# Output sums of the first output pair kept in SBUF, one queue step per job

## The chip, the cores and the metric

The kernel runs on one core of a Trainium2 chip. The metric is the device time of one execution in microseconds (us). Three runs of the kernel before took 1672.77, 1674.2 and 1676.46 us, with a median of 1674.2.

## The reference

Two layers run over a sequence of 512 rows of width 2048 (float32). Each layer normalises its input, multiplies it by one wide input matrix, hands the columns to a gated-linear-attention (GLA) group of 4 heads and a chunked-attention group of 8 heads, normalises and gates each head's output, concatenates both groups, multiplies by an output matrix, normalises and adds the input:

```python
h = rmsnorm(x, g_pre)
z = h @ w_in
gq, gk, gv, gg, ga, aq, ak, av, ag = split_columns(z)
...
o_gla = rmsnorm(o_gla, ...) * silu(gg)      # 1024 columns, 4 heads of 256
o_att = rmsnorm(o_att, ...) * silu(ag)      # 1024 columns, 8 heads of 128
y = jnp.concatenate([o_gla, o_att], axis=-1) @ w_out
return x + rmsnorm(y, g_post)
```

The change concerns the last product, `@ w_out`, and the way its left operand reaches TensorE.

## The kernel before

**Products.** The weights are cut into blocks of 512 columns: 14 of `w_in` and 4 of `w_out` for each layer. Float32 precision is had from a split: an operand is a high part (ScalarE's copy to fp32r) and a low part (VectorE's difference), and a product is the sum of three matmuls, high by high, high by low, low by high. The weights' parts are the tiles `wh` and `wl`, with four and three buffers.

**Pairs of blocks.** Most blocks are multiplied two at a time by `fast_gemm`, with a scheme of Strassen's kind: seven products, P1 to P7, on sums of quarter blocks instead of eight on quarter blocks. Each product has four steps over the contraction (0 to 3), so that a pair is 28 *jobs* of 12 matmuls each. A job loads its weights (`Job.load`), adds them where its product needs a sum and casts the high part (`high`), and makes the low part (`low`). Loads run up to five jobs ahead of the matmuls, the other steps three to four (`ahead`). The order of the jobs is written out by hand; for the first output pair it is `PROD_OUT`:

```python
PROD_OUT = order("10 20 11 21 12 13 50 51 60 61 22 23 52 53 62 63 30 31 32 33 70 71 72 73 40 41 42 43")
LEFT = {"P5": "S1", "P6": "S2", "P3": "S4", "P7": "S3", "P4": "A22"}
```

"50" is step 0 of P5. `LEFT` names the left operand: P5, P6, P3 and P7 need a sum, S1, S2, S4 or S3, of quarters of the activations. The four steps of an output pair take the GLA heads in the order `OC` = 2, 3, 0, 1.

**The output sums.** For each step the quarters are a11 and a21 (attention, first and second half of the rows, read from DRAM by `out_parts`) and a12 and a22 (GLA head, first and second half, written by `turn_gla`). S1 = a21 - a22, S2 = S1 - a11, S4 = a12 + S2, S3 = a11 - a21. `make_sums` makes the four of one head after another, as soon as both halves of the head are there; each is one VectorE operation and a split. The result is put into one of the slots g0 to g3, written to DRAM (`so_d`, tile name oS in the profile, on POOL's queue), and read again by the job that needs it into the ring `sa` (four buffers, on SP's queue, line 175). The parts of the four heads share two sets of slots, g9/g10 and g12/g13.

**What runs around it.** Before the output pair the pair PAIRS[5] makes the GLA gates. Its consumer (`gg_consume`) gates the heads, and `turn_gla` transposes them on TensorE (line 1123), 8 or 11 queue steps later. Steps of this kind stand in `tasks` (generators, one step at a time) and `delayed` (a countdown). `Pace` runs `rate` of these steps behind each job; it was 3 in the gate pair and in the output pair. A task was also `residual_rows`, which loads the layer's input rows (12 loads on POOL's queue), needed at the end of the layer in `finish_token` (line 1262). The first output pair gives columns 0 to 1023. The other 1024 come from `std_gemm` in layer 0 and from a second `fast_gemm` (W23) in layer 1, which needs the same sums.

**Order on the engines.** The program's order is not the last word: a planner replays the program against its own durations and sets each engine's order from that. `tc.issue_after(last_cast[0])` keeps a sum's copy behind the newest weight cast on ScalarE.

Of the kernel before, what the change touches and what calls it, by code (L numbers as in the profile page):

```python
# [7 lines left out]
F32 = mybir.dt.float32  # L8
# [3 lines left out]
ALU = mybir.AluOpType  # L12
# [21 lines left out]
def hybrid_trunk(  # L34
# [60 lines left out]
    sa_d = [{(n, c): dram([P, 1024], f"{n}{l}{c}") for n in ("S1", "S2", "S3", "S4", "A22") for c in range(4)} for l in range(L)]  # L95
    so_d = [{(n, c): dram([P, 1024], f"o{n}{l}{c}") for n in ("S1", "S2", "S3", "S4") for c in range(4)} for l in range(L)]
    oa_d = [{(h, c): dram([P, 1024], f"oa{l}{h}{c}") for h in range(2) for c in range(4)} for l in range(L)]
# [39 lines left out]
    class Job:  # L137
# [14 lines left out]
        def load(self):  # L152
            k, c, p, b0, b1 = self.kind, self.c, self.pair, self.b0, self.b1
            end = b0 >= NB_IN and k != "std"
            if end:
                c = OC[c]
            top, bottom = (c + 4, c) if end else (c, c + 4)
            if k == "std":
                self.raw = self.fetch(rtile("raw"), b0, c)
            elif k == "P1":  # L160
                p["H", self.c] = self.fetch(rtile("H"), b0, top)
            elif k == "P5":
                p["r", self.c] = self.fetch(rtile("raw"), b1, top)
            elif k == "P6":
                p["r", self.c] = self.fetch(rtile("raw"), b1, bottom)
            elif k == "P7":
                p["r", self.c] = self.fetch(rtile("raw"), b0, top)
            elif k == "P2" or (k == "P4" and end):
                p["r", self.c] = self.fetch(rtile("raw"), b0, bottom)
            sums = (so_d if end else sa_d)[self.l]  # L170
            src = sums.get((LEFT.get(k), c))
            if src is not None and not (k == "P5" and b0 == AV0):
                until(lambda: k == "P4" or (id(sums), LEFT[k], c) in written)
                self.a = rtile("sa", (2, 512), F32R)
                nc.sync.dma_start(flat(self.a), src)
# [140 lines left out]
    def fast_gemm(l, pair, consume, rate=0.0, skip=0, feature_major=False, after=None, end=False, lag=0, ops=A):  # L316
# [38 lines left out]
        def matmuls(job, k, c, ts):  # L355
            a = job.a
            if a is None:
                key = {"P1": (0, 0, c), "P2": (1, 0, c), "P4": (1, 1, c), "P5": ("S1", c)}[k]
                until(lambda: key in ops)
                a = ops[key]  # L360
# [327 lines left out]
    def layer(l):  # L688
# [416 lines left out]

        parts = {}

        def out_parts(c):
            if c not in parts:
                halves = [slot(tag, [2, 512]) for tag in (("g9", "g10"), ("g12", "g13"))[c % 2]]  # L1110
                parts[c] = [halves[0][:, 0, :], halves[0][:, 1, :], halves[1][:, 0, :], halves[1][:, 1, :]]
                for half in range(2):
                    nc.sync.dma_start(
                        parts[c][2 * half].rearrange("p (k n) -> p k n", k=2),
                        of_att[l][c][:, :, half * 256 : (half + 1) * 256],
                    )
            return parts[c]

        def turn_gla(h, p):
# [17 lines left out]
            og[p, h] = op  # L1137
            O[1, p, OC.index(h)] = op

        def gla_heads(j, gvh, gvl):  # L1140
# [41 lines left out]

        def ready_parts(c):
            return parts[c] if (0, c) in og and (1, c) in og else None

        def gv_consume(j, h, t, src, comb):
# [11 lines left out]
        def gg_consume(j, h, t, src, comb):  # L1198
            until(lambda: len(gla_done) == 4)
            sg = t2()  # L1200
            nc.scalar.activation(sg, settled(src, comb), AF.Silu)
            for i in range(2):
                dst = normed[2 * j + i, h][:, t, :]
                nc.vector.tensor_tensor(out=dst, in0=dst, in1=sg[:, i * 256 : (i + 1) * 256], op=ALU.mult)
                if t:
                    delayed.append([8 + 3 * i, lambda hd=2 * j + i: turn_gla(hd, h)])

        tasks.append(make_sums(so_d[l], ("g0", "g1", "g2", "g3"), ready_parts, chunks=OC))
        fast_gemm(l, PAIRS[5], gg_consume, rate=3, after=fetch_operands)
# [12 lines left out]

        def load_gain(n):
            gp = t2()
            src = g_post[l, n * W : (n + 1) * W]
# [15 lines left out]
        def out_evac(n):  # L1241
            gp = load_gain(n)

# [33 lines left out]

        def residual_rows():
            for half in range(2):
                xs.append(load_tokens(half, x_src, nc.gpsimd))  # L1280
                yield

        tasks.append(residual_rows())

        def out_consume(n):
            gains = [load_gain(n + j) for j in range(2)]

            def f(j, h, t, src, comb):
                o = 2 * h + t
                project(o, n + j, comb(t2()), gains[j])  # L1290
# [7 lines left out]

        fast_gemm(l, W01, out_consume(0), rate=3, end=True, ops=O)
        drain()  # L1300
        if last:
            fast_gemm(l, W23, out_consume(2), rate=3, end=True, lag=3, ops=O)
# [68 lines left out]
```

## Time and profile before

| | |
|---|---|
| median of three runs | 1674.2 us |
| the profiled execution, its time | 1678.37 us |
| its span, first to last instruction | 1676.5 us |
| mean granted TensorE clock | 0.986 |
| TensorE busy | 1622.6 us (97%) |
| VectorE busy | 1261.3 us (75%) |
| ScalarE busy | 908.0 us (54%) |
| POOL busy | 142.5 us (8%) |
| moved by DMA | 451.34 MB, mean 269 GB/s |

In the profile PE is TensorE, PEld its weight loads, DVE VectorE, ACT ScalarE, SP and POOL the engines whose queues issue most of the DMAs. A row of the waits reads: engine, tile and line, what it waited for, total us, times, longest us. A row of the chain reads: start, duration, what. A row of the timeline reads: start, duration, engine, line, operation, output tile <- input tiles, shape, count, and in brackets the idle time before it with what ended it. A row of the windows reads: stretch, its length, then busy us and count of each engine, the granted clock as a share of full speed, the DMA engines' busy share and GB/s. A row of a group ends with busy us and mean ns of one, then idle time. A row of the DMA issues gives count, KB each, and median us to landing. Times are us from the span's start.

### The profile page before, as it was taken

The numbers are of one execution on the slowest core, as the hardware profiler recorded it, in microseconds if no ns is written. First come the engines' busy times: TensorE is split into PE (matmuls) and PEld (weight loads), VectorE is DVE, ScalarE is ACT, GpSimd is POOL, SyncE is SP. The second block draws the span as 40 slices with busy tenths as digits, with TensorE's granted clock in tenths as the row PEclk, the third lists the DMA queues.
The fourth block names the chain that finished last, engine by engine and source line by source line (L and its number), as shares of the span: only waits on it lengthen the run. The fifth ranks groups of instructions, "written<-read, shape, count | busy, mean of one in ns | idle before, by whom it ended". The sixth has DMA issues, their size and how long they took to land.

```text
span 1676.5 us, 24715 instructions
## 1 busy us (share of the span) xinstructions
PE 1622.6 (97%) x8986; PEld 1387.4 (83%) x8986; DVE 1261.3 (75%) x1639; ACT 908.0 (54%) x1494; POOL 142.5 (8%) x216
## 2 busy tenths in 40 slices
PE   9999999999999999599999999999999999996996
PEld 7888999998887778488888889999988877775884
DVE  5977777777687869685786577776776878796878
ACT  7554445666554557354774444455665545573542
POOL 0110000010110111100122000000100000111002
PEclk9999999999999999799999999999999999997998
DMA  8788685875859688986789496858758586889965
GB/s 339 269 343 312 221 294 185 301 267 190 301 191 334 206 278 317 329 326 207 242 280 400 160 323 213 300 179 277 259 191 286 199 317 215 290 322 332 346 225 201
DMA packets 137528, 451.34 MB, mean 269 GB/s; under 512 B 14836, under 2 KB 27508, under 8 KB 137408
## 3 DMA queue, kind: packets, MB, share of 16 engines
q1 hardware_dynamic: 117792, 380.77, 65.6%
q0 software_dynamic: 19040, 67.92, 10.5%
q8 instruction: 71, 1.16, 0.3%
q10 hardware_dynamic: 576, 1.08, 0.2%
q14 instruction: 49, 0.40, 0.1%
HBM read 388.10 MB, written 61.62 MB: 268 GB/s over the span
## 4 chain that ended last, share of the span: by engine, by line
PE 85%; DMA 7%; issue 4%; DVE 2%; POOL 1%; ACT 0%; SPq 0%; DVEq 0%; POOLq 0%; ACTq 0%
PE mm L381 44%; PE mm L302 16%; PE mm L371 16%; DMA raw<-in_w_dram 3%; PE ax L891 2%; DMA sa<-oS 1%; DMA oS<-g 1%; DVE wl L199 1%; PE ax L1072 1%; PE ax L874 1%; PE ax L711 1%; PE ax L1044 1%; PE ax L381 1%; PE ax L855 1%; PE ax L854 1%
## 5 line engine op out<-in xcount | busy, mean ns | idle before, releaser
L381 PE MATMUL mm<-wh,sa 128*128 128x512 f32 x1600 | 523.6, 398 | 34.6 <-DMA sa<-oS 34.6
L199 DVE TENSOR_TENSOR wl<-raw,wh 128x1024 fp32r<-128x1024 f32 (+1 forms) x253 | 306.8, 1216 | 125.8 <-PE mm L381 63.2
L191 ACT CAST wh<-raw 128x1024 fp32r<-128x1024 f32 (+1 forms) x253 | 265.3, 1053 | 244.7 <-PE mm L381 75.8
L381 PEld LDWEIGHTS mm<-wh,sa 128*128 128x128 f32 x1600 | 304.0, 190 | 110.3 <-issue 37.2
L191 ACT CAST wh<-H 128x1024 fp32r<-128x1024 f32 x240 | 251.4, 1050 | 209.9 <-PE mm L381 88.9
L199 DVE TENSOR_TENSOR wl<-H,wh 128x1024 fp32r<-128x1024 f32 x240 | 292.3, 1220 | 88.7 <-PE mm L381 26.2
L381 PE MATMUL mm<-wl,sa 128*128 128x512 f32 x800 | 315.9, 395 | 0.0
L371 PE MATMUL mm<-sa,wh 128*128 128x256 f32 x1280 | 236.9, 285 | 0.5 <-DMA sa<-S 0.5
L381 PE MATMUL mm<-wh,a 128*128 128x512 f32 x608 | 200.4, 394 | 0.0
L371 PEld LDWEIGHTS mm<-sa,wh 128*128 128x128 f32 x1280 | 199.6, 191 | 0.7 <-ACT wh L191 0.6
L371 PE MATMUL mm<-sa,wl 128*128 128x256 f32 x640 | 181.5, 284 | 0.7 <-DVE wl L199 0.6
L381 PEld LDWEIGHTS mm<-wl,sa 128*128 128x128 f32 x800 | 152.2, 190 | 29.9
L185 DVE TENSOR_TENSOR H<-H,raw 128x1024 f32<-128x1024 f32 x132 | 160.4, 1219 | 6.1 <-DMA raw<-in_w_dram 4.8
L381 PEld LDWEIGHTS mm<-wh,a 128*128 128x128 f32 x608 | 113.2, 188 | 23.2
L421 POOL TENSOR_TENSOR sm<-sm,mhalf 128x2 f32<-128x2 f32 (+2 forms) x42 | 54.7, 1302 | 904.6 <-DVE sm L901 452.9
L371 PEld LDWEIGHTS mm<-sa,wl 128*128 128x128 f32 x640 | 122.4, 191 | 1.3 <-DVE wl L199 1.1
L187 DVE TENSOR_TENSOR raw<-H,raw 128x1024 f32<-128x1024 f32 x60 | 73.5, 1224 | 62.2 <-DMA raw<-in_w_dram 61.9
L381 PE MATMUL mm<-wl,a 128*128 128x512 f32 x304 | 120.2, 395 | 0.0
L371 PE MATMUL mm<-a,wh 128*128 128x256 f32 x512 | 95.2, 285 | 0.0
L302 PE MATMUL mm<-wh,a 128*128 128x512 f32 x288 | 91.7, 390 | 0.0
L333 ACT COPY ev<-mm 128x512 f32<-128x512 f32 x96 | 55.9, 584 | 65.9 <-PE mm L381 49.2
L302 PE MATMUL mm<-wh,g 128*128 128x512 f32 x240 | 81.9, 391 | 0.0
(227 smaller groups left out, 2348.3 us busy)
## 6 DMA issues: line engine op xcount, KB each, us to landing
raw<-in_w_dram SPq DMA_DIRECT2D x323, 512.0 KB, 4.8
sa<-S SPq DMA_DIRECT2D x184, 512.0 KB, 4.3
H<-in_w_dram SPq DMA_DIRECT2D x60, 512.0 KB, 4.9
sa<-A SPq DMA_DIRECT2D x48, 512.0 KB, 6.1
sa<-oS SPq DMA_DIRECT2D x48, 512.0 KB, 5.8
S<-g POOLq DMA_DIRECT2D x32, 512.0 KB, 8.6
oS<-g POOLq DMA_DIRECT2D x32, 512.0 KB, 7.4
oa<-g POOLq DMA_DIRECT2D x12, 512.0 KB, 5.7
```

The lines of the kernel that those rows point to most:

```text
L185: nc.vector.tensor_tensor(out=h, in0=h, in1=r, op=ALU.add)
L187: nc.vector.tensor_tensor(out=r, in0=h, in1=r, op=ALU.subtract)
L191: last_cast[0] = nc.scalar.copy(self.wh[:, z, :], src[:, z, :]).ins
L199: nc.vector.tensor_tensor(out=self.wl[:, z, :], in0=self.src[:, z, :], in1=self.wh[:, z, :].bitcast(F32), op=ALU.subtract)
L302: nc.tensor.matmul(pss[o], a(part, kk, o) if callable(a) else a[:, part, t], rhs[:, kk, :], start=(i == 0 and kk == 0 and m == 0), stop=(i ...
L333: nc.scalar.copy(e, src[t])
L371: nc.tensor.matmul(dst, lhs[:, kk, f], a[:, part, tok], start=(fresh and kk == 0 and m == 0 and ft % 2 == 0), stop=(c == 3 and kk == 1 and ...
L381: nc.tensor.matmul(out_ps[t], a[:, part, tok], rhs[:, kk, :], start=(fresh and kk == 0 and m == 0), stop=(c == 3 and kk == 1 and m == 2), ...
L421: nc.gpsimd.tensor_tensor(out=out_r, in0=v, in1=mhalf[:, : v.shape[-1]], op=ALU.pow)
L711: nc.tensor.matmul(ps[0:96, half * 256 : (half + 1) * 256], wga[kt // 10][:, kt % 10, :], op[:, i, (kt % 2) * 256 : (kt % 2 + 1) * 256], s ...
L854: nc.tensor.matmul(ps[:, :n], self.qh[:, t], self.kl[:, :n], start=False, stop=False)
L891: nc.tensor.matmul(o, self.pt[i][:, j * P : (j + 1) * P], av[hd // 4, j // 2][:, j % 2, (hd % 4) * P : (hd % 4 + 1) * P], start=(j == 0), ...
```

## The change

The sums of the first output pair are made by a new generator, `output_sums`, in the order in which the products use them: S1 and S2 of the first two heads, of the other two, then S4 and S3 of all four. Each step of the generator makes one sum. The sums stay in SBUF, in slots g0 to g3 and in the ring `sa`, and a job takes them from there (the table `ops`); a sum that replaces another waits until that one's job has passed (`used`). In layer 1 each is also written to DRAM for the second pair. All four heads keep parts of their own: heads 2 and 3 in g9/g10 and g12/g13, head 0 in g16/g17, head 1 in four buffers of `t2`. The gains of the first output pair are loaded into the `bias` buffers once all heads are turned. Heads 0 and 1 are turned after 6, 7, 3 and 4 queue steps instead of 8 and 11. The output pair runs one queue step per job instead of three, and the residual rows are loaded behind it.

```diff
-    so_d = [{(n, c): dram([P, 1024], f"o{n}{l}{c}") for n in ("S1", "S2", "S3", "S4") for c in range(4)} for l in range(L)]
+    so_d = {(n, c): dram([P, 1024], f"o{n}{c}") for n in ("S1", "S2", "S3", "S4") for c in range(4)}
...
-            sums = (so_d if end else sa_d)[self.l]
+            sums = so_d if end else sa_d[self.l]
             src = sums.get((LEFT.get(k), c))
-            if src is not None and not (k == "P5" and b0 == AV0):
+            if src is not None and b0 != NB_IN and not (k == "P5" and b0 == AV0):
...
-                key = {"P1": (0, 0, c), "P2": (1, 0, c), "P4": (1, 1, c), "P5": ("S1", c)}[k]
+                key = {"P1": (0, 0, c), "P2": (1, 0, c), "P4": (1, 1, c)}.get(k) or (LEFT[k], c)
                 until(lambda: key in ops)
...
-        parts = {}
+        parts, gains = {}, []
+
+        PARTS = {2: ("g9", "g10"), 3: ("g12", "g13"), 0: ("g16", "g17")}
 
         def out_parts(c):
             if c not in parts:
-                halves = [slot(tag, [2, 512]) for tag in (("g9", "g10"), ("g12", "g13"))[c % 2]]
-                parts[c] = [halves[0][:, 0, :], halves[0][:, 1, :], halves[1][:, 0, :], halves[1][:, 1, :]]
+                if c in PARTS:
+                    halves = [slot(tag, [2, 512]) for tag in PARTS[c]]
+                    parts[c] = [z[:, i, :] for z in halves for i in range(2)]
+                else:
+                    parts[c] = [t2() for _ in range(4)]
...
+        used = set()
+
+        def output_sums():
+            def put(name, i, src, tag=None):
+                op = O[name, i] = slot(tag, [2, 512], F32R) if tag else rtile("sa", (2, 512), F32R)
+                with tc.issue_after(last_cast[0]):
+                    split(op[:, 0, :], op[:, 1, :], src)
+                if last:
+                    nc.gpsimd.dma_start(so_d[name, OC[i]], flat(op))
+                    written.add((id(so_d), name, OC[i]))
+
+            def sub(dst, a, b):
+                nc.vector.tensor_tensor(out=dst, in0=a, in1=b, op=ALU.subtract)
+
+            for i0 in (0, 2):
+                for name in ("S1", "S2"):
+                    for i in (i0, i0 + 1):
+                        while (1, OC[i]) not in og:
+                            yield
+                        a11, _, a21, a22 = parts[OC[i]]
+                        sub(a22, *((a21, a22) if name == "S1" else (a22, a11)))
+                        put(name, i, a22, None if i0 else f"g{i + 2 * (name == 'S2')}")
+                        yield
+            for name in ("S4", "S3"):
+                for i in range(4):
+                    while (("P5", "P6")[i // 2], i % 2 + 2 * (name == "S3")) not in used or (0, OC[i]) not in og:
+                        yield
+                    a11, a12, a21, a22 = parts[OC[i]]
+                    if name == "S4":
+                        nc.vector.tensor_tensor(out=a12, in0=a12, in1=a22, op=ALU.add)
+                        put(name, i, a12, f"g{i}")
+                    else:
+                        sub(a11, a11, a21)
+                        put(name, i, a11)
+                    yield
...
             O[1, p, OC.index(h)] = op
+            if len(og) == 8:
+                for n in range(2):
+                    gains.append(tmp.tile([P, W], F32, tag="bias", name=nm("bias"), bufs=2))
+                    load_gain(n, gains[n])
...
         def gg_consume(j, h, t, src, comb):
-            until(lambda: len(gla_done) == 4)
+            if t == 0:
+                until(lambda: len(gla_done) == 4 and (j or {(1, 2), (1, 3)} <= set(og)))
+                for i in range(2):
+                    out_parts(2 * j + i)
...
-                    delayed.append([8 + 3 * i, lambda hd=2 * j + i: turn_gla(hd, h)])
+                    delayed.append([(8 + 3 * i if j else 6 + i if h == 0 else 3 + i), lambda hd=2 * j + i: turn_gla(hd, h)])
 
-        tasks.append(make_sums(so_d[l], ("g0", "g1", "g2", "g3"), ready_parts, chunks=OC))
+        tasks.append(output_sums())
...
-        def residual_rows():
-            for half in range(2):
-                xs.append(load_tokens(half, x_src, nc.gpsimd))
-                yield
-
-        tasks.append(residual_rows())
...
-            gains = [load_gain(n + j) for j in range(2)]
+            if n:
+                gains[:] = [load_gain(n + j, t2()) for j in range(2)]
 
             def f(j, h, t, src, comb):
+                until(lambda: len(gains) == 2)
...
-        fast_gemm(l, W01, out_consume(0), rate=3, end=True, ops=O)
+        fast_gemm(l, W01, out_consume(0), rate=1, after=lambda k, c: used.add((k, c)), end=True, ops=O)
         drain()
+        xs.extend(load_tokens(half, x_src, nc.gpsimd) for half in range(2))
```

More of the change, by code (lines that the diff above doesn't have):

```diff
@@ L1181, in fetch_operands @@
                     nc.sync.dma_start(flat(op_att[0, i]), oa_d[l][0, i])
-        def ready_parts(c):
-            return parts[c] if (0, c) in og and (1, c) in og else None
         def gv_consume(j, h, t, src, comb):
@@ L1221, in layer, with load_gain @@
         YS = (("a122", "a123", "g8", "g11"), ("g0", "g1", "g2", "g3"))
-        def load_gain(n):
-            gp = t2()
+        def load_gain(n, gp):
             src = g_post[l, n * W : (n + 1) * W]
@@ L1241, in out_evac @@
         def out_evac(n):
-            gp = load_gain(n)
+            gp = load_gain(n, t2())
             def f(o, ps):
```

## The prediction

> **What bounds the kernel now.** I read the page first, then TensorE's waits, then the chain of waits in order of time, then the timeline and the windows of the stretches that the chain named.
>
> ```profile
> PE 1622.6 (97%) x8986; PEld 1387.4 (83%) x8986; DVE 1261.3 (75%) x1639; ACT 908.0 (54%) x1494; POOL 142.5 (8%) x216
> PE mm L381 <- DMA sa<-oS: 34.6, 7, 13.8
> PE mm L381 <- DVE wl L199: 2.6, 3, 1.1
> ```
>
> TensorE is the bound over the whole span, so only two things can make the kernel shorter: less matmul time, or less of the 53.9 us (1676.5 - 1622.6) in which TensorE has none. Of these, 34.6 us in 7 waits have one releaser: a load of an output sum (oS) from DRAM into a ring tile (sa). VectorE's low parts (wl), the other thing a product waits for, cost 2.6 us. The timeline shows that six of the seven lie in the first output pair, three in each layer:
>
> ```profile
> 673.44 0.50 PE L381 MATMUL mm<-wh,sa 128*128 128x512 f32 x1 [3.42 <-DMA sa<-oS]
> 689.98 0.47 PE L381 MATMUL mm<-wh,sa 128*128 128x512 f32 x1 [1.01 <-DMA sa<-oS]
> 706.83 0.77 PE L381 MATMUL mm<-wh,sa 128*128 128x512 f32 x1 [13.82 <-DMA sa<-oS]
> ...
> 1507.69 0.50 PE L381 MATMUL mm<-wh,sa 128*128 128x512 f32 x1 [1.36 <-DMA sa<-oS]
> 1524.68 0.77 PE L381 MATMUL mm<-wh,sa 128*128 128x512 f32 x1 [3.09 <-DMA sa<-oS]
> 1540.15 0.77 PE L381 MATMUL mm<-wh,sa 128*128 128x512 f32 x1 [11.01 <-DMA sa<-oS]
> ```
>
> That is 18.25 us in layer 0 and 15.46 in layer 1. The chain tells what the long ones are made of:
>
> ```profile
> 102.02 76.27 PE mm L381 x336
> ...
> 688.72 10.40 DMA oS<-g
> 699.17 7.53 DMA sa<-oS
> ```
>
> The sum was in SBUF by 688.72. It was then written to DRAM (10.40) and read back (7.53): a round trip of 18 us for data that never had to leave. The first row is a measure: 28 jobs of 12 matmuls, with no gap, take 76.27 us, 2.72 a job. Now the output pair of layer 0 (648.92 to 750.55), that of layer 1, and parts of the first:
>
> ```profile
> core 0: us, PE busy (x) PEld busy (x) DVE busy (x) ACT busy (x) POOL busy (x), PEclk, DMA share, GB/s
> 648.92:750.55 101.63, 83.37 (x355) 67.68 (x354) 79.57 (x96) 50.19 (x75) 11.88 (x23) 0.90 0.92 338
> 1485.25:1583.87 98.62, 83.17 (x356) 67.63 (x355) 79.08 (x95) 49.45 (x75) 11.86 (x23) 0.91 0.95 360
> 648.92:672.00 23.08, 21.10 (x101) 17.15 (x99) 23.08 (x33) 15.77 (x27) 5.49 (x11) 1.00 0.98 359
> 672.00:706.83 34.83, 18.55 (x72) 14.56 (x73) 25.15 (x32) 13.96 (x21) 6.39 (x12) 0.78 0.91 322
> 706.83:750.55 43.72, 43.72 (x182) 35.97 (x183) 31.34 (x32) 20.46 (x28) 0.00 (x0) 0.94 0.91 339
> 640.00:648.92 8.92, 8.92 (x41) 7.37 (x40) 8.92 (x13) 6.08 (x9) 1.00 (x2) 1.00 0.71 246
> ```
>
> The same 336 matmuls are here busy for 83.4 us, since the granted clock is 0.78 around the gaps and 0.94 behind them, and there are 16 transposes more. VectorE is busy for 79.6 us of the pair: that is more than TensorE's undisturbed time, and it is what to look at next.
>
> **The round trip removed.** The transposes first: four take 0.35 us, from 661.66 to 662.01, so 16 take 1.4.
>
> ```profile
> 661.66 0.60 PE L1123 MATMUL ax<-cst,bias 128*128 128x128 f32 x4
> 662.01 0.48 PE L381 MATMUL mm<-wl,a 128*128 128x512 f32 x1
> ```
>
> Undisturbed, the pair is 76.27 + 1.4 = 77.7 us. Against the measured 101.63 and 98.62 that is 23.9 and 20.9 us, 44.8 in all: 18.25 and 15.46 of idle time, 5.7 (83.37 - 77.7) and 5.5 of matmuls at a lower clock. This is the most that the change can bring. The Trainium skill, TensorE: Matmul & The Clock Gate, Part 1, says that the clock halves after about 3.4 us without work and comes back after about 3.4 us of it. By that a long gap costs about 1.7 us more than itself, at most two gaps in a layer count, and the most would be about 40.5 (estimate) instead of 44.8. The clock rows agree in kind; their 5.7 and 5.5 are larger than that estimate, and I keep them.
>
> **VectorE, which then decides.** A job's low part and its weight sum are 128x1024 operations, a sum and its low part 128x512 ones. They follow each other at 1.14 (two in 2.28) and 0.60 us:
>
> ```profile
> 661.18 2.35 DVE L199 TENSOR_TENSOR wl<-H,wh 128x1024 fp32r<-128x1024 f32 x2
> 663.46 0.68 DVE L106 TENSOR_TENSOR a<-g,a 128x512 fp32r<-128x512 f32 x1
> ...
> 743.57 1.23 DVE L199 TENSOR_TENSOR wl<-H,wh 128x1024 fp32r<-128x1024 f32 x1
> 744.71:750.55 5.84, 5.84 (x27) 4.85 (x26) 3.68 (x6) 2.88 (x5) 0.00 (x0) 1.00 0.67 236
> L542 DVE TENSOR_TENSOR g<-g,g 128x512 f32<-128x512 f32 x4 | 2.7, 683 | 0.0
> L539 DVE TENSOR_TENSOR g<-g,g 128x512 f32<-128x512 f32 x3 | 2.1, 685 | 0.0
> L533 DVE TENSOR_TENSOR g<-g 128x512 f32<-128x512 f32 x2 | 1.4, 684 | 0.0
> L536 DVE TENSOR_TENSOR g<-g,g 128x512 f32<-128x512 f32 x2 | 1.4, 683 | 0.0
> ```
>
> The arithmetic of the 16 sums stays: one tensor operation and one split each. Eleven fall into the pair of layer 0 now (4 + 3 + 2 + 2). In the new generator S1 and S2 of the first two heads come before it, since they need only the second halves of heads 2 and 3, and twelve fall behind: 1.2 us more. Behind the last low part that a product of the pair needs (743.57) come 3.7 us that belong to what follows (the row of 744.71 to 750.55). So VectorE must do 79.6 + 1.2 - 3.7 = 77.1 us, and one job of 2.72 us follows. At full occupancy the pair then takes 79.8 us, 2.1 more than TensorE alone.
>
> How full can it be? From 640 to 672 VectorE was busy without a break (8.92 of 8.92 and 23.08 of 23.08 us), on the same mixture of low parts, weight sums and output sums, and TensorE lost nothing to it before the DRAM wait at 670. The other end is 31.34 of 43.72 us (72%), but there its idle time is TensorE's pace; by it the pair would take 77.1 / 0.72 + 2.7 = 110. I take 97%, near the first, since VectorE then has a backlog to work off and waits seldom: 77.1 / 0.97 + 2.7 = 82.2 us. The gains are 101.6 - 82.2 = 19.4 and 98.6 - 82.2 = 16.4: 35.8 us.
>
> The sums themselves come in time. S1 of the third head is put one job ahead of the pair and first used by its thirteenth, S4 ten jobs and S3 eight jobs ahead: 22 us or more, against 2.4 for the step. One step per job instead of three costs nothing for that reason.
>
> **Edits with small prices.** The transposes of the last two heads come 3 to 7 queue steps behind the product instead of 8 to 11. If they were issued straight away, TensorE would wait for the gating in VectorE (655.64 below, 6.7 us behind 648.92); the planner of the order put them behind other matmuls before (661.66), and may again. Between 0 and 6.7 a layer I take 0: such a wait only moves VectorE's backlog forward. Four t2 buffers of eight now hold the parts of head 1 and two fewer hold gains; a consumer takes two for some 2 us, so this is 0.
>
> The 16 loads in each layer and the 16 writes in layer 0 go (512 KB each). The residual rows, 12 loads on POOL's queue, move behind the pair:
>
> ```profile
> sa<-oS SPq DMA_DIRECT2D x48, 512.0 KB, 5.8
> g<-in_x_dram POOLq DMA_DIRECT2D x6, 512.0 KB, 7.6
> 655.64 0.42 DVE L1204 TENSOR_TENSOR sg<-sg,t 128x256 f32<-128x256 f32 x1
> 795.11 1.27 DVE L1262 SCALAR_TENSOR_TENSOR g<-a,sm,g 128x1024 f32<-128x1024 f32 x1
> 750.55:776.00 25.45, 25.45 (x114) 21.05 (x113) 15.38 (x16) 12.90 (x18) 0.00 (x0) 1.00 0.65 219
> 1583.87:1609.00 25.13, 25.13 (x113) 20.81 (x112) 21.80 (x22) 13.95 (x19) 0.00 (x0) 1.00 0.60 198
> ```
>
> They are first needed 44.6 us behind the pair (795.11 - 750.55) and land in 7.6, twelve of them in some 15 to 25 us. The DMA engines are 0.60 to 0.65 busy there, so the weights have room beside them: 0 to 2 us, taken as 0. The Trainium skill, DMA: Bandwidth & Descriptors, Issuing engines are not separate DMA queues, speaks against the move: POOL's loads run on the same 16 DMA engines as the weights. By it the twelve loads take turns with the weights of the next pair. The rows leave a third of the DMA engines' time for that. A wait is added on SP's queue: the two gains go into the bias buffers, which come free with head 0's transposes, and the parts of heads 0 and 1 are loaded at P2's end of the pair before. Behind them on SP stand the weights of the output pair. These are fetched up to five jobs (13.6 us) ahead; the gains can be held no longer than the 6.7 us above, so this is 0 unless the weights' landing of 4.8 us doubles too. Who waits for the gains is the first consumer, eleven jobs later. In layer 1 the 16 writes stay, for the second pair.
>
> **The sum.** The profiled execution took 1678.4 us (span 1676.5); less 35.8 that is 1642.6. The median of the runs shown, 1674.2, is 4.2 lower, and less 35.8 it is **1638.4 us**. What a measurement can tell from no change is about 0.2%, 3.3 us.
>
> **The rivals.**
> 1. VectorE becomes the bound outright. If waits for casts, loads and copies keep it at 86% in the pair, the pair takes 77.1 / 0.86 + 2.7 = 92.4; gains 9.2 + 6.2 = 15.4, and 1658.8 us. For it: 77.1 us must pass in order through one engine, and low parts stand behind sums. Against: the unbroken 32 us.
> 2. Slower. Each sum's ScalarE copy is queued behind the newest weight cast, which waits for weights; VectorE's low part of the sum waits for the copy, and every later weight low part waits behind it. With a landing of 4.8 us less one job, 2.1 a sum, 24 sums in both pairs cost 50.4 us against 44.8: 1679.8 us. It decides from 1.9 us a sum (44.8 / 24). Against it: the old sums had the same rule, and their low parts waited 14.0 us in 16 cases, 1.5 at most.
>
> ```profile
> raw<-in_w_dram SPq DMA_DIRECT2D x323, 512.0 KB, 4.8
> DVE g L106 <- ACT g L105: 14.0, 16, 1.5
> ```
>
> 3. Nothing comes of it: the wait for a load is replaced by one of the same length for the sum itself, 1674.2. Against it: the sum was in SBUF 18 us ahead of its matmul.
> 4. VectorE hides altogether, by its lead of two jobs and by sums put later: 44.8, so 1629.4.
>
> **How the numbers follow.** The forecast (pairs of 80 to 86 us, 1634 to 1646) has 0.62; rival 1, to 1658.8, 0.20; rival 2, 0.08; rival 3, 0.03; rival 4, 0.07. The range from 1629.4 to 1658.8 leaves rivals 2 and 3 out. Faster 0.89, within 0.2% 0.03, slower 0.08.
>
> **What would show it.** In the changed kernel's profile: no oS load in TensorE's waits within the first output pair; no dip of the granted clock there; pairs of 80 to 86 us; VectorE over 93% busy in them; waits of products for wl larger than now. Wrong would be: a new wait of TensorE of over 5 us in the pair (for a sum, a transpose or a weight), or pairs longer than 90 us.

## The result, and the profile after

The changed kernel takes 1657.9 us (median of 4 runs, 1657.6 to 1662.7), the kernel before, beside it, 1675.3. The ratio is 0.9901 with a 95% interval of 0.9873 to 0.9928: faster by 17.4 us, less than half of the 35.8 us that the forecast took off. The page of the changed kernel (span 1656.1 us), TensorE's waits and the DMA issues:

```profile
PE 1623.9 (98%) x8986; PEld 1386.1 (84%) x8986; DVE 1260.1 (76%) x1639; ACT 905.3 (55%) x1494; POOL 131.7 (8%) x200
PE mm L381 <- DVE wl L199: 13.3, 12, 2.1
PE mm L381 <- ACT wh L191: 4.0, 3, 2.1
sa<-oS SPq DMA_DIRECT2D x16, 512.0 KB, 5.2
```

The loads of output sums fell from 48 to 16, and none is left among what TensorE waits for: the 34.6 us are gone. In their place stand waits for weights, for the low part (wl: 2.6 us before, 13.3 now) and for the cast (wh, 4.0). Windows on the first output pair of each layer, from its first matmul to its last, and on two stretches of layer 1; behind the times stand the busy times of PE, PEld, DVE, ACT and POOL, the granted clock, the DMA share and GB/s:

```profile
647.38:732.95 85.57, 79.87 (x354) 64.46 (x353) 78.69 (x94) 48.81 (x75) 4.85 (x9) 1.00 0.59 203
1467.09:1562.29 95.20, 85.74 (x353) 67.10 (x352) 77.15 (x92) 47.93 (x74) 12.26 (x23) 0.95 0.76 273
...
1474.00:1478.00 4.00, 4.00 (x14) 3.04 (x13) 4.00 (x8) 0.93 (x2) 1.06 (x2) 0.61 1.02 278
1508.40:1512.50 4.10, 4.06 (x10) 2.79 (x10) 1.43 (x3) 0.00 (x0) 0.53 (x1) 0.58 1.00 388
```

Cut in the same way, the pairs of before are 101.5 and 98.1 us. Layer 0 gained 15.9, layer 1 only 2.9, and together that is 18.8 of the 20.4 us by which the span fell. So the question is why layer 1's pair still takes 95.2. Its gaps in the timeline of TensorE:

```profile
1473.54 0.50 PE L381 MATMUL mm<-wl,a 128*128 128x512 f32 x1 [1.79 <-DVE wl L199]
...
1508.44 0.50 PE L381 MATMUL mm<-wl,sa 128*128 128x512 f32 x1 [2.01 <-DVE wl L199]
...
1514.69 0.74 PE L381 MATMUL mm<-wh,sa 128*128 128x512 f32 x2 [2.11 <-ACT wh L191]
1515.95 0.80 PE L381 MATMUL mm<-wl,sa 128*128 128x512 f32 x1 [0.52 <-DVE wl L199]
```

Each gap is followed by matmuls at a lower clock (0.61 and 0.58 in the last two windows above, 0.64 from 1514.60 to 1519.00), which is why PE is busy for 85.7 us there and 79.9 in layer 0. Layer 0's pair has the first of these gaps too, as long and at the same place, and there the clock stayed at 1.00:

```profile
653.84 0.50 PE L381 MATMUL mm<-wl,a 128*128 128x512 f32 x1 [1.79 <-DVE wl L199]
...
653.50:657.50 4.00, 3.67 (x17) 3.02 (x18) 4.00 (x9) 1.89 (x3) 0.53 (x1) 1.00 1.00 259
```

The chain of waits around 1508 (start, us, what) leads back to a weight load:

```profile
1502.07 10.17 DMA raw<-in_w_dram
1512.26 1.24 DVE H L185
1513.59 1.05 ACT wh L191
1514.67 1.24 DVE wl L199
```

A load that takes 10.17 us hurts only if it started late. SP's queue shows that it did. Its timeline, its waits in the same stretch (1476 to 1502.5), and a row of VectorE's timeline:

```profile
1481.28 0.33 SPq L1270 DMA_DIRECT2D bias<-in_g_post_dram  x1
1499.73 0.33 SPq L149 DMA_DIRECT2D raw<-in_w_dram  x1
...
SPq L149 <- DVE wl L199: 22.5, 3, 15.8
...
1498.48 1.22 DVE L199 TENSOR_TENSOR wl<-raw,wh 128x1024 fp32r<-128x1024 f32 x1
```

For 18.4 us SP fetched nothing (1481.28 is a load of gains): the next weight load got its tile of the ring `raw` when VectorE had made a low part from it, at 1499.70. The ring has four tiles. P6's loads of steps 0 and 1 keep two of them until P3 uses them; the plain weights of P2's steps 2 and 3 are in the other two. This is the place to test.

### The profile page after: what moved, and what is told of

Read it like the earlier page. It is cut to its first block, busy times and chain, and to the rows that moved or that the text cites. A ratio compares the mean times of both kernels' runs of the same rounds, so it can differ in the third digit from the quotient of the medians.

```text
span 1656.1 us, 24554 instructions
## 1 busy us (share of the span) xinstructions
PE 1623.9 (98%) x8986; PEld 1386.1 (84%) x8986; DVE 1260.1 (76%) x1639; ACT 905.3 (55%) x1494; POOL 131.7 (8%) x200
## 4 chain that ended last, share of the span: by engine, by line
PE 88%; DVE 5%; DMA 3%; issue 2%; ACT 0%; POOL 0%; DVEq 0%; ACTq 0%; POOLq 0%
PE mm L381 42%; PE mm L371 18%; PE mm L302 16%; DMA raw<-in_w_dram 3%; PE ax L891 2%; DVE wl L199 2%; PE ax L381 1%; PE ax L1072 1%; PE ax L874 1%; PE ax L711 1%; PE ax L1044 1%; DVE H L185 1%; PE ax L855 1%; PE ax L854 1%; PE ax L853 1%
## 5 line engine op out<-in xcount | busy, mean ns | idle before, releaser
L381 PE MATMUL mm<-wh,sa 128*128 128x512 f32 x1472 | 479.5, 396 | 4.0 <-ACT wh L191 4.0
L381 PEld LDWEIGHTS mm<-wh,sa 128*128 128x128 f32 x1472 | 277.1, 189 | 72.5 <-issue 8.3
L381 PE MATMUL mm<-wl,sa 128*128 128x512 f32 x736 | 290.1, 394 | 5.6 <-DVE wl L199 5.5
L381 PEld LDWEIGHTS mm<-wl,sa 128*128 128x128 f32 x736 | 139.1, 189 | 35.5 <-DVE wl L199 8.5
L185 DVE TENSOR_TENSOR H<-H,raw 128x1024 f32<-128x1024 f32 x132 | 160.1, 1217 | 8.5 <-DMA raw<-in_w_dram 7.4
L371 PE MATMUL mm<-a,wh 128*128 128x256 f32 x512 | 95.2, 285 | 0.0
L381 PE MATMUL mm<-wh,g 128*128 128x512 f32 x288 | 92.2, 395 | 0.0
```

The costliest lines, as they stand in the source:

```text
L185: nc.vector.tensor_tensor(out=h, in0=h, in1=r, op=ALU.add)
L371: nc.tensor.matmul(dst, lhs[:, kk, f], a[:, part, tok], start=(fresh and kk == 0 and m == 0 and ft % 2 == 0), stop=(c == 3 and kk == 1 and ...
L381: nc.tensor.matmul(out_ps[t], a[:, part, tok], rhs[:, kk, :], start=(fresh and kk == 0 and m == 0), stop=(c == 3 and kk == 1 and m == 2), ...
```

## The experiments

Theories named in the expectations, in the order in which they came up. **A**: the raw tiles that P6 keeps for P3 leave two of four for all other loads, so a late load's landing lies on the path. **B**: VectorE is the bound, as rival 1 had it. **C**: the shorter countdown puts ScalarE's copies of the turned heads ahead of a weight cast; the casts come late, the raw tiles come free late. **D**: the early transposes and copies cost by themselves. **E**, the reason behind C: the PSUM ring `ax` has four tiles. Heads 0 and 1 take four in `turn_gla`, P2's accumulators two (`acc["Z"] = [aux(), aux()]`), and who claims first goes first.

All kernels are the changed one with the edit shown, `before_short` excepted. Ratios are to the kernel before, with 95% intervals. The kernel before was run again beside each group and took 1675.3 to 1678.8 us there, so kernels of different groups are better compared by their ratios than by their medians. A pair's time is from one profiled execution; executions of one kernel differ by 1 to 7 us, and a difference of a few us between two pairs may be that.

| kernel | median us | ratio | pair, layer 0 | pair, layer 1 |
|---|---|---|---|---|
| before | 1675.3 | 1 | 101.5 | 98.1 |
| changed | 1657.9 | 0.9901 [0.9873, 0.9928] | 85.6 | 95.2 |
| p3load | 1647.5 | 0.9819 [0.9786, 0.9852] | 85.3 | 87.2 |
| swap | 1655.7 | 0.9867 [0.9837, 0.9898] | 92.2 | 89.4 |
| hold | 1653.3 | 0.9858 [0.9821, 0.9896] | 87.6 | 84.9 |
| turn | 1642.0 | 0.9780 [0.9751, 0.9810] | 80.9 | 83.7 |
| split | 1648.0 | 0.9822 [0.9784, 0.9860] | 83.1 | 85.9 |
| before_short | 1663.7 | 0.9913 [0.9885, 0.9941] | 93.9 | 93.4 |
| turn_p3 | 1645.1 | 0.9805 [0.9768, 0.9843] | 82.4 | 84.2 |
| turn_pool | 1662.9 | 0.9909 [0.9879, 0.9940] | 89.8 | 94.9 |
| turn_light | 1642.2 | 0.9781 [0.9758, 0.9804] | 80.3 | 83.8 |
| turn_heavy | 1650.2 | 0.9828 [0.9802, 0.9854] | 86.8 | 88.6 |
| turn_rate3 | 1647.5 | 0.9812 [0.9790, 0.9835] | 83.3 | 86.0 |
| turn_hold | 1642.9 | 0.9788 [0.9766, 0.9809] | 80.1 | 80.4 |
| zmem | 1646.6 | 0.9828 [0.9804, 0.9853] | 83.3 | 85.5 |
| turn_h0short | 1644.6 | 0.9817 [0.9791, 0.9843] | 81.6 | 85.5 |
| turn_h1short | 1655.5 | 0.9877 [0.9845, 0.9908] | 88.5 | 89.1 |

### First four: where the late load comes from

**p3load** fetches P3's weights anew in the first output pair, so that P6's raw tiles come free.

```diff
                 p["r", self.c] = self.fetch(rtile("raw"), b0, top)
+            elif k == "P3" and b0 == NB_IN:
+                p["r", self.c] = self.fetch(rtile("raw"), b1, bottom)
```

> P3's jobs of the first output pair fetch their weights anew (4 loads of 512 KB a layer more), so that P6's raw tiles need not be held until P3. Theory A (the weights' ring: P6's four raw tiles are held for P3, two of the four raw buffers are left for ten loads, and each late load's landing stands on the path): the hold of 18 us on SP's queue goes, the pair of layer 0 falls from 85.7 to 80-82 us, that of layer 1 from 96.4 to 82-86, 1642 to 1647 us. Theory B (VectorE is the bound of the pair, as predicted, and late loads only follow from it): the same VectorE work, 2 MB more by DMA a layer, pairs unchanged within 1 us, 1657 to 1660 us.

Layer 1 fell by 8.0 us to 87.2. Layer 0 stayed, where A had it fall to 80 to 82. Held tiles matter, as A says, but it shows in layer 1 alone, where the loads land slowly. B does not fit.

**swap** moves the 16 writes of the sums from layer 1 to layer 0.

```diff
-                if last:
+                if not last:
                     nc.gpsimd.dma_start(so_d[name, OC[i]], flat(op))
-                    written.add((id(so_d), name, OC[i]))
+                written.add((id(so_d), name, OC[i]))
```

> The 16 writes of the sums to DRAM move from layer 1 to layer 0; layer 1's second pair multiplies the sums of layer 0 (that part of the result is left wrong), its loads and times stay. Theory A: landing of weights beside the writes is what separates the layers: layer 0's pair goes from 85.7 to 90-96, layer 1's from 96.4 to 85-88 us, total 1655 to 1659. Theory B: both within 1 us of what they were, 1657 to 1659.

The long pair moves along in part: layer 0 goes from 85.6 to 92.2, layer 1 from 95.2 to 89.4. The writes are worth some 6 us of a pair, and they explain part of the difference between the layers, not what both have in common.

**hold** keeps each residual load back until the pair's end, by a one-column copy into its tile.

```diff
             for z in row:
+                nc.vector.tensor_copy(z[:, 0:1], behind[:, 1:2])
                 q.dma_start(z, src[t * P : (t + 1) * P, o : o + z.shape[-1]])
...
-        xs.extend(load_tokens(half, x_src, nc.gpsimd) for half in range(2))
+        xs.extend(load_tokens(half, x_src, nc.gpsimd, ssy[3]) for half in range(2))
```

> Each of the 12 residual loads waits for the last statistic of the pair's last token (a VectorE copy of one column before each, 12 a layer), so that none of them runs inside the pair. Theory A: the weights' landing of 10.2 and 8.8 us in layer 1 gets shorter by the residual rows' share of the traffic: layer 1's pair 91-95 instead of 96.4, layer 0's unchanged, 1652 to 1657. Theory B: no gain, 12 small operations more on VectorE, 1658 to 1661.

Layer 1's pair fell by 10.3 us in the profiled execution, layer 0's rose by 2.0, and the execution as a whole is 4.1 us shorter, so part of the gain is lost again behind the pair; the median is 4.6 us lower, inside the intervals. In the changed kernel, then, the residual loads are not behind the pair at all. They stand behind it in the program, but the planner of the order moves them forward, as POOL's timeline of the changed kernel shows:

```profile
1500.59 0.53 POOL L1132 DMA_DIRECT2D oS<-g  x1 [5.95 <-DVE g L106]
1501.20 0.53 POOL L1132 DMA_DIRECT2D oS<-sa  x1
1501.72 0.54 POOL L456 DMA_DIRECT2D g<-x_mid  x1
```

These loads and writes run beside the load of 10.17 us, which started at 1502.07. SP's hold is not dear by itself: its longest wait for a raw tile is 16.1 us in layer 0's pair, as long as in layer 1, and that pair is 9.6 us shorter; in hold it is 16.3 us in layer 1's pair of 84.9.

**turn** puts back the old countdown of heads 0 and 1.

```diff
-                    delayed.append([(8 + 3 * i if j else 6 + i if h == 0 else 3 + i), lambda hd=2 * j + i: turn_gla(hd, h)])
+                    delayed.append([8 + 3 * i, lambda hd=2 * j + i: turn_gla(hd, h)])
```

> Heads 0 and 1 are turned after 8 and 11 queue steps again, everything else as changed. Theory A: the wait of 1.8 us for a low part at the start of each pair goes, nothing else moves: 1653 to 1657. Theory B: the sums start later and VectorE's work is pressed into less time, pairs 1 to 4 us longer: 1659 to 1665.

Both theories missed, by more than 10 us: no kernel of the study is faster, and it is 15.9 us under the changed one. Windows on its two pairs:

```profile
648.27:729.13 80.86, 79.15 (x354) 64.60 (x353) 78.71 (x94) 49.22 (x75) 4.83 (x9) 1.00 0.62 216
1461.66:1545.32 83.66, 80.39 (x353) 63.84 (x352) 77.74 (x93) 48.16 (x74) 12.26 (x23) 1.00 0.83 303
```

No clock dip, VectorE busy for 97% of layer 0's pair (78.71 of 80.86). The pairs are shorter by 4.7 and 11.5 us, 16.2 together. The same writes and residual loads run in these pairs (POOL's counts are the same), and the layers differ by only 2.8 us. So the countdown comes first, and the late loads that A names make it dear in layer 1. By the ratios turn is 20 us under the changed kernel, by the medians 15.9.

### Second four: which part of the countdown

**split** transposes early, but puts ScalarE's copies and the split of the second halves of heads 0 and 1 off by 5 and 7 steps.

```diff
+            if wait:
+                delayed.append([wait, lambda: turned_gla(h, p, ps)])
+            else:
+                turned_gla(h, p, ps)
...
-                    ..., lambda hd=2 * j + i: turn_gla(hd, h)])
+                    ..., lambda hd=2 * j + i, i=i: turn_gla(hd, h, 0 if j or h == 0 else 5 + 2 * i)])
```

> Heads 0 and 1, second halves: the transposes on TensorE keep the short countdown (3 and 4 queue steps), the copies on ScalarE and the split get the old one (8 and 11). Theory C (the short countdown puts ScalarE's copies of turned heads ahead of a weight cast; the casts then run 4 to 6 us late, the raw tiles come free 7 us late, and the weights' landing is on the path): part of the 16 us comes back, 1644 to 1653 us. Theory D (the early transposes on TensorE are the cost: its wait of 2 us and the order behind it): as changed, 1655 to 1660.

1648.0 is within C's figures and below D's: the transposes stay early, and most of the 16 us comes back. But C's reason doesn't show. ScalarE's third weight cast comes 9.1 us into either pair, as it does in the changed kernel's layer 0 (10.0 in layer 1), and TensorE has the same gap of 1.79 us. What split gives back comes later in the pair; how, no run shows.

**before_short** is the kernel before with the new countdown alone.

```diff
-                    delayed.append([8 + 3 * i, lambda hd=2 * j + i: turn_gla(hd, h)])
+                    delayed.append([(8 + 3 * i if j else 6 + i if h == 0 else 3 + i), lambda hd=2 * j + i: turn_gla(hd, h)])
```

> The kernel before with nothing but the short countdown. Theory C: its casts are late as well, but TensorE waits for the round trip of the sums anyway: within 3 us of before, ratio 0.998 to 1.002. Theory D: the wait on the transposes adds to the round trip, 3 to 8 us longer, ratio 1.002 to 1.005.

C and D were both wrong here: it is faster than before, by 13.5 us (1677.2 beside it). TensorE's waits tell why:

```profile
PE mm L381 <- DMA sa<-oS: 9.3, 5, 3.7
PE mm L381 <- DVE wl L199: 9.0, 7, 2.1
PE mm L381 <- ACT wh L191: 5.7, 3, 5.1
```

Heads turned earlier give their sums earlier, and 25.3 of the 34.6 us of the round trip disappear under other work. The price shows beside it: wl (2.6 us before) and wh (under 0.3) rise to 14.7 us together. The countdown and the sums kept in SBUF are two remedies for one wait. Where the sums stay in SBUF, the countdown brings only its price.

**turn_p3** is turn with the edit of p3load.

> The old countdown, and P3's jobs fetch their weights anew. Theory A (two raw buffers for ten loads are the next limit): pairs from 80.9 and 83.7 to 79-81, 1635 to 1640 us. Theory B (VectorE is the bound once the countdown is long): unchanged, 1640 to 1644.

No gain: 1645.1, above the figures of both theories, against 1642.0, and the intervals overlap. With the old countdown the held raw tiles cost nothing that can be measured.

**turn_pool** is turn with the tensor operations of the 16 sums on POOL, to take work off VectorE.

```diff
-                nc.vector.tensor_tensor(out=dst, in0=a, in1=b, op=ALU.subtract)
+                nc.gpsimd.tensor_tensor(out=dst, in0=a, in1=b, op=ALU.subtract)
```

> The old countdown, and the 16 sums of a layer (the subtraction or addition, not the split) on POOL instead of VectorE: 16 x 0.6 = 9.6 us less on VectorE in and around each pair. Theory B: pairs of 78 to 80 us, 1632 to 1638. Theory A: the weights' ring holds the pair, 1640 to 1644; longer if POOL takes so long for a sum that a product waits for it.

Both theories missed again: 21 us slower than turn. Groups of layer 0's pair, first of turn_pool, then of turn (busy us, mean ns):

```profile
L199 DVE TENSOR_TENSOR wl<-raw,wh 128x1024 fp32r<-128x1024 f32 x14 | 20.2, 1446 | 0.2 <-PE mm L381 0.2
L185 DVE TENSOR_TENSOR H<-H,raw 128x1024 f32<-128x1024 f32 x12 | 17.9, 1488 | 0.1
L1136 POOL TENSOR_TENSOR g<-g,g 128x512 f32<-128x512 f32 x4 | 6.2, 1553 | 2.1 <-DVE sa L106 2.1
L1153 POOL TENSOR_TENSOR g<-g,g 128x512 f32<-128x512 f32 x3 | 5.4, 1811 | 0.0
```

```profile
L199 DVE TENSOR_TENSOR wl<-raw,wh 128x1024 fp32r<-128x1024 f32 x14 | 17.0, 1217 | 0.0
L185 DVE TENSOR_TENSOR H<-H,raw 128x1024 f32<-128x1024 f32 x12 | 14.6, 1219 | 0.1
L1136 DVE TENSOR_TENSOR g<-g,g 128x512 f32<-128x512 f32 x4 | 2.7, 683 | 0.0
```

A sum takes on average 1.6 and 1.8 us in the two groups on POOL against 0.68 on VectorE, and VectorE's own operations beside it grow from 1217 to 1446 ns. VectorE is busy longer than with the work it gave away (84.3 us in the pair against 78.7). The Trainium skill, SBUF — State Buffer, Who interferes with whom, says that a VectorE instruction with two inputs from SBUF contends with a GpSimd (POOL) instruction that reads SBUF; these rows agree with it.

### Third four: is VectorE the limit once the countdown is back?

**turn_light** and **turn_heavy** take eight operations of about 0.6 us a layer from VectorE, or add eight.

```diff
# turn_light
-                        nc.vector.tensor_tensor(out=a12, in0=a12, in1=a22, op=ALU.add)
...
-                        sub(a11, a11, a21)
# turn_heavy
+                    nc.vector.tensor_tensor(out=a11, in0=a11, in1=a11, op=ALU.max)
```

> The old countdown; the additions of S4 and the subtractions of S3 are left out (8 operations of 0.6 us a layer; the products use the unsummed quarters). Theory B (with the old countdown VectorE paces the pair, 77.1 us of work at 93 to 97%): pairs 2 to 4 us shorter than 80.9 and 83.7, 1634 to 1639 us. Theory A (loads pace it): within 1 us a pair, 1640 to 1643.

> The old countdown, and in each of the eight steps of S4 and S3 one more VectorE operation of the same size that changes nothing (maximum of a11 with itself): 4.8 us more a layer. Theory B: pairs 3 to 5 us longer, 1647 to 1653 us. Theory A: within 2 us a pair, 1642 to 1646.

Windows on the pairs of turn_light, then of turn_heavy:

```profile
648.93:729.27 80.34, 79.16 (x354) 64.52 (x353) 74.53 (x86) 48.95 (x75) 4.88 (x9) 1.00 0.64 215
1462.52:1546.31 83.79, 80.62 (x353) 63.94 (x352) 73.65 (x85) 48.28 (x74) 12.31 (x23) 1.00 0.80 302
```

```profile
649.18:736.01 86.83, 81.34 (x354) 65.60 (x353) 83.35 (x102) 49.29 (x75) 4.86 (x9) 0.98 0.60 200
1469.11:1557.68 88.57, 81.71 (x353) 64.99 (x352) 81.43 (x100) 48.40 (x74) 12.27 (x23) 0.98 0.79 285
```

Of some 9 us more on VectorE, 8.3 come out in the median, as B has it, though turn's interval touches this one; of some 9 us less, nothing does, as A has it. With the old countdown the two engines are balanced: in layer 0 TensorE is busy for 79.15 of turn's 80.86 us and for 79.16 of turn_light's 80.34. The next microsecond on VectorE costs, a microsecond less gains nothing.

**turn_rate3** sets the pace in the pair back to three queue steps per job, **turn_hold** joins turn and hold.

```diff
-        fast_gemm(l, W01, out_consume(0), rate=1, after=...
+        fast_gemm(l, W01, out_consume(0), rate=3, after=...
```

> The old countdown and three queue steps per job in the output pair instead of one, so the sums come earlier in the program. Theory C (copies of sums and turned heads ahead of weight casts make the weights late): pairs 1 to 5 us longer, 1644 to 1654 us. Theory B: the same VectorE work, 1640 to 1644.

> The old countdown, and the residual loads held back to the end of the pair by a one-column VectorE copy each. Theory A: layer 1's pair nears layer 0's (83.7 to 81-82), 1638 to 1641 us. Theory B: 12 small operations more on VectorE, 1641 to 1645.

At three steps the median is 5.6 us longer (1647.5, in C's range), though the intervals still overlap: one step per job costs nothing that can be measured, and may gain. Holding the residual loads back does not move the median here (1642.9), though layer 1's pair in the profiled execution is 3.3 us shorter (80.4).

### Last three: the countdown itself, or the order it brings?

**zmem** keeps the short countdown. Only P2's two accumulators are claimed first, by a one-column memset each.

```diff
+            if (j, h, t) == (0, 0, 0):
+                zs[:] = [aux(), aux()]
+                for z in zs:
+                    nc.vector.memset(z[:, 0:1], 0.0)
...
-                acc["Z"] = [aux(), aux()]
+                acc["Z"] = zs[:] if b0 == NB_IN else [aux(), aux()]
```

**turn_h0short** and **turn_h1short** apply the short countdown to one half only: the first halves of heads 0 and 1 (6 and 7 steps), or the second (3 and 4).

```diff
# turn_h0short
+                    delayed.append([(8 + 3 * i if j or h else 6 + i), lambda hd=2 * j + i: turn_gla(hd, h)])
# turn_h1short
+                    delayed.append([(8 + 3 * i if j or h == 0 else 3 + i), lambda hd=2 * j + i: turn_gla(hd, h)])
```

> The changed kernel with its short countdown. Only the two PSUM tiles of P2's accumulators (ring ax, four buffers) are claimed before the turned heads' tiles, by a one-column memset of each. Nothing of the result changes. In the written order the third weight cast of the pair then stands ahead of ScalarE's copies of the turned heads, as with the long countdown. Theory C with E (the ring's claim puts P2 and so the cast behind the copies; the transposes themselves cost nothing): pairs of 80 to 86 us, 1640 to 1648. Theory D (early transposes and copies cost whatever the order of the cast is): as the changed kernel, 1654 to 1660.

> The changed kernel with the short countdown for the first halves of heads 0 and 1 (6 and 7 steps) and the old one for their second halves (8 and 11). Two of the four ring buffers are then free when P2 begins. Theory C with E: as with the old countdown for all, 1639 to 1646. Theory D: half of the two early turns is left, so about half of the 16 us, 1648 to 1654.

> The changed kernel with the short countdown for the second halves of heads 0 and 1 alone (3 and 4 steps; the first halves 8 and 11). In the written order one turned head's copy stands ahead of the third weight cast, the other's behind it with the tiles claimed in a different order. Theory C with E: between, and nearer to the changed kernel: 1648 to 1657. Theory D: half of the cost, 1648 to 1654.

All three times came out as C with E has them. ScalarE's timeline at the start of layer 1's pair, first of the changed kernel (the pair starts at 1467.09), then of zmem (1468.90):

```profile
1470.05 1.05 ACT L191 CAST wh<-H 128x1024 fp32r<-128x1024 f32 x1 [0.94 <-ACT t L1246]
1471.45 0.84 ACT L1173 ACTIVATE g<-ax,gcol 128x256 f32<-128x256 f32 x2 [0.35 <-PE ax L1164]
1472.18 0.84 ACT L1173 ACTIVATE t<-ax,gcol 128x256 f32<-128x256 f32 x2
1472.89 0.63 ACT L105 CAST a<-g 128x512 fp32r<-128x512 f32 x1
1473.40 0.64 ACT L105 CAST a<-t 128x512 fp32r<-128x512 f32 x1
1477.12 1.05 ACT L191 CAST wh<-H 128x1024 fp32r<-128x1024 f32 x1 [3.07 <-PE mm L381]
```

```profile
1472.32 1.05 ACT L191 CAST wh<-H 128x1024 fp32r<-128x1024 f32 x1 [1.40 <-issue]
1475.31 1.05 ACT L191 CAST wh<-H 128x1024 fp32r<-128x1024 f32 x1 [1.94 <-DVE wl L199]
1476.26 0.83 ACT L1174 ACTIVATE g<-ax,gcol 128x256 f32<-128x256 f32 x2
1476.99 0.84 ACT L1174 ACTIVATE t<-ax,gcol 128x256 f32<-128x256 f32 x2
```

The third weight cast runs 10.0 us into the pair in the changed kernel, behind the copies of two turned heads, and 6.4 in zmem, ahead of them (6.4 in turn as well). But, against C, the copies do not hold it up: they end at 1474.04, and the row of the cast shows a wait of 3.07 us for a matmul. What differs first is TensorE's own order. The rows of the changed kernel, of turn (its pair starts at 1461.66) and of zmem, with the low part (wl) that P1's step 1 needs:

```profile
1472.27 1.22 DVE L199 TENSOR_TENSOR wl<-H,wh 128x1024 fp32r<-128x1024 f32 x1
1478.01 0.60 PE L381 MATMUL ax<-wh,g 128*128 128x512 f32 x1
...
1466.84 1.21 DVE L199 TENSOR_TENSOR wl<-H,wh 128x1024 fp32r<-128x1024 f32 x1
1464.87 0.71 PE L381 MATMUL ax<-wh,g 128*128 128x512 f32 x2
...
1469.13 0.62 PE L382 MATMUL ax<-wh,g 128*128 128x512 f32 x2
```

The low part is begun 5.2 us into the pair in the changed kernel and in turn alike. In turn and zmem TensorE has P2's step 0 (`ax<-wh,g`) to do meanwhile, from 3.2 and 0.2 us into the pair, and has no gap there. In the changed kernel it turns the heads, goes on to P1's step 1, waits 1.79 us for that low part (the gap at 1473.54 above), and comes to P2 only 10.9 us into the pair. It is so in both pairs of every run: P2 starts at most 3.3 us into the pair with the old countdown of the second halves and in zmem, and 9.4 to 11.0 us into it with their short countdown, behind a gap. That is E, the order of claims, without C's copies. One thing stays mixed: zmem also moves the turned heads' first copies from 4.4 to 7.4 us into the pair, where turn has them, so it doesn't tell the claim from the early turning.

SP's waits for raw tiles in the corresponding stretch of turn and of zmem:

```profile
SPq L149 <- DVE wl L199: 12.0, 3, 8.1
```

```profile
SPq L149 <- DVE wl L199: 13.6, 3, 8.5
```

Against 22.5 and 15.8 in the changed kernel. Claiming two PSUM tiles first gives back 11.3 of the 16 us (1657.9 to 1646.6; 12 of 20 by the ratios) with the countdown untouched. What is left to turn, 4.6 us or 8 by the ratios, is at the edge of the intervals. It is the second halves that do it: alone they cost nearly everything (1655.5), the first halves little (1644.6, and the intervals overlap turn's).

## Why the prediction was right and wrong

**The round trip (right).** The waits for oS are gone, and where nothing else came in their place (turn, layer 0) the clock stayed at 1.00.

**The pair at 82.2 us with VectorE at 97% (right for everything but one edit).** Turn is the whole change except the countdown; its pairs take 80.9 and 83.7, 82.3 on average, and it gains 35.0 us in the pairs against the 35.8 of the sum. That the average meets 82.2 so closely is luck: the sum has both layers alike, and they differ by 2.8 us. VectorE is at 97% in layer 0 and 93% in layer 1. The reason is half right: TensorE needs 79.2 us busy, not 77.7, so VectorE has TensorE close beside it, and relieving it gains nothing (turn_light).

**The failed step: the countdown at 0.** The prediction put it "between 0 and 6.7 a layer" and took 0, since "such a wait only moves VectorE's backlog forward". It measures 4.7 us in layer 0 and 11.5 in layer 1, 15.9 in the medians. I had looked for TensorE waiting for a transpose. The price came another way: the turned heads claimed tiles of a PSUM ring ahead of P2's accumulators, so that TensorE came to P2's step 0 10.9 us into the pair instead of 3.2, with a gap of 1.79 us where that work had been; with P2's claim put first (zmem, which also turns the heads later), 11.3 us came back. What follows in layer 1 (raw tiles free late, loads late, further gaps with a slower clock) is read from the waits of one execution; p3load bears out the held tiles, swap and hold the traffic beside the loads. That ScalarE's copies delay the weight cast is not shown, and what the late copies of split gain stays open. The edit moved instructions on TensorE, ScalarE and in the PSUM ring; I costed it on one engine.

**"Fetched up to five jobs (13.6 us) ahead" (wrong).** That is the program's limit. The ring's four raw tiles set a shorter one, and SP was held for up to 15.8 us in layer 1 (8.1 in turn). The condition that I named, a landing twice 4.8 us, then came about: 10.17 us on the path in layer 1.

**Residual rows behind the pair (wrong as to the place).** Nine of their ten instructions (the prediction counted twelve) are issued inside it in either layer; they are POOL's x9 in layer 0's window. Without them layer 1's pair is 10.3 us shorter while the weights are late (hold); with the old countdown the median gains nothing (turn_hold).

**Rival 1** had this time, 1658.8, and its figure: VectorE is busy for 155.8 of the two pairs' 180.8 us, 86%. It named "casts, loads and copies" as what holds VectorE up and gave that 0.20. Its head, VectorE as the bound, does not hold: its work in the pairs is the same in turn, which takes 16 us less.

**What would show it.** No oS waits, and larger waits for wl: as said. Pairs of 80 to 86: in layer 0 (85.6), not in layer 1. VectorE over 93%: no, 92% and 81%. No dip of the clock: so in layer 0, not in layer 1 (0.95). TensorE's waits for weights add up to 9.3 us in layer 1's pair, the longest 2.1. A pair over 90 us was named as the sign of an error, and it was one.

## What to carry to other kernels

When a change brings a step forward, write down every queue and every ring of buffers that the step passes (PSUM tiles too), and look up whose claim it overtakes. Two remedies for one wait don't add up: test each alone and both together, since the second may be all price. How far ahead loads run is read from the load queue's waits for buffers, not from the look-ahead in the program.

## What the runs showed of the hardware

Behind gaps of 1.79 and 2.01 us in layer 1's pair the granted clock was about 0.6 for the next 4 us (the windows and the timeline of the changed kernel above); TensorE's busy time is 85.7 us there against 79.9 in layer 0's pair. A gap of this length can do that and need not: behind the 1.79 us of layer 0's pair the clock was 1.00. What decides, no run here shows. The Trainium skill, TensorE: Matmul & The Clock Gate, Part 1, ties the drop to an idle window of about 3.4 us. Here no single gap was that long, so a short gap can be dearer than the prediction's estimate by that rule.

With twelve 128x512 operations on POOL in one pair, VectorE's operations beside them took longer, one group by a fifth (1217 to 1446 ns, turn_pool).
